# Token sums held behind each head's root, the last gate tile in the branches' banks, the small projection amid the first keys, and the decay's minimum in a row of its own

## The chip, the core and the metric

The kernel runs on one core of one Trainium2 chip. A core has a matrix engine (TensorE, "PE" in the profile, its weight loads "PEld"), VectorE (DVE), ScalarE (ACT), GpSimd (POOL) and SyncE (SP), each with an instruction stream of its own that runs in order, and 16 DMA engines. The metric is the device time of one execution in microseconds; less is better.

## The reference

One layer of a hybrid decoder: a norm, one wide projection, two token-mixing branches that are gated and merged, an output projection, and a gated FFN with a causal convolution. There are 1024 tokens of 1024 channels, and 16 meta tokens in front of them (1040 in all).

```python
proj = h @ w_in + b_in                 # queries, keys, values, gates, and the small columns g_lr, m_i, m_f
log_a = log_sigmoid(g_lr @ gla_w_gate + gla_b_gate) / 16
o_gla = gla_chunked(q, k, v, log_a)    # 4 heads: gated linear attention, chunks of 64 tokens
o_ml  = mlstm_chunked(mq, mk, mv, log_i, log_f)         # 4 heads: matrix memory
y = sigmoid(gate_a) * (o_gla @ w_branch_gla) + sigmoid(gate_b) * (o_ml @ w_branch_ml)
x1 = x + y @ w_out
out = rms_norm(x1 + (silu(conv(x1n @ w_up)[gate]) * conv(x1n @ w_up)[up]) @ w_down)
```

`log_sigmoid(z)` is worked out as min(z, 0) - ln(1 + exp(-|z|)). Each head's output goes through a norm of its own, which needs one number per token, (mean of squares + eps) to the power -1/2; that power is called the head's root here.

## The kernel before

Every float32 matrix product is made of three matmuls on split operands (high by high, low by high, high by low part). So a tile `wr_x` is a weight as it was loaded, `wH_x` its high part, which ACT writes, and `wL_x` the low part, which DVE writes (lines 109 and 110). `xH` and `xL` are the input, split the same way.

The kernel has stages. The heads stage runs to about 640 us: for head s = 0 to 7, `key_query_proj(s)` and `value_proj(s)` are the main stream of matmuls, and `main` lets the generators of the head before (`gla` for heads 0 to 3, `mlstm` for 4 to 7) and a closing generator `post` advance by 1.15 steps for each step of the main stream. `post` scales and turns a finished head's rows (`ot`, `of`), and stores them. Then come the gates (`piece`, tiles Vg, Xg, Yg, Zg and gu, to about 938 us), the two branches' products (`bg` and `bm`, to about 1126 us), the output projection, and the FFN. A tile scheduler sets each engine's order from the order of the code, from priorities (`hp`), and from `issue_after`, which holds an instruction in the schedule until a named one has been issued. Each engine then runs its list strictly in order, DMA issues included.

Around the change:

- A head's finish. DVE writes `rs{s}v` (line 91), POOL takes the root `rs{s}r` (line 93), and in heads 4 to 7 DVE multiplies the result by `rc` (line 937). On DVE the next in order behind that are the value tiles `v` (line 208), which read the matmuls of `value_proj` out of their PSUM banks.
- Token sums. `post` of heads 3 to 6 calls `token_sums`: eight POOL operations (lines 468 and 471) of 128x514 on tiles `xa` and `xb`, and eight DMA issues from POOL's queue (line 483) that store them for the FFN's stage. `half_load` and `half_sums` (lines 496 and 502) do the like for a piece of a weight. `xa` and `xb` take their buffers from a tag of two, which is also that of `KT`, the turned keys of the next head (lines 765 and 872).
- Decay. For heads 0 to 3 `decay` multiplies the small projection by the gate's weights into three PSUM tiles `pre` (128x346 or 348, from a tag of three buffers that the scores, the states and others share), ACT makes ln(1 + exp(-|z|)) in `la` in the steps Abs (line 620), Exp and Ln, DVE takes min(z, 0) - la from the PSUM tiles in three operations (line 624) and makes the running sum `bc` (line 627). From `bc` follow the factors `pk` of the scores `sc` of the first head, level by level.
- The small projection. `key_query_proj(0)` runs keys and queries of head 0 and keys of head 1 together, and then the small columns (`uk["lr"]`, weights `w_lr`) as 72 matmuls; `decay(0)` is called behind it.
- The last gate tile. `merge_gate_b(7)` (its matmuls are `pe`, its output `gb`) runs at the end of the gates stage, each third of it in a bank of its own (`pe7_0`, `pe7_342`, `pe7_684`), and ACT takes each third out with a copy (line 456). Then `load_o` loads the first branch's operand, of which ACT writes the high part `ogH` (line 1207, eight operations) and DVE the low part `ogL` (line 1208), and the branch's products start.

Of the kernel before, what the change touches and what calls it, by code (L numbers as in the profile page):

```python
# [17 lines left out]
P = 128  # L18
# [27 lines left out]
def hybrid_kernel(ctx, tc, x, meta, norm_mix, w_in, b_in, gla_w_gate, gla_b_gate, gla_norm,  # L46
# [38 lines left out]
    warm = const.tile([P, 1], F32, name="warm")  # L85
    nc.scalar.activation(warm, one1, AF.Exp)

    def rstd_of(ss, n, w, pool, name):

        v = pool.tile([P, w], F32, name=name + "v", tag="rv", bufs=4)  # L90
        nc.vector.tensor_scalar(v, ss, 1.0 / n, EPS, OP.mult, OP.add)
        r = pool.tile([P, w], F32, name=name + "r", tag="rr", bufs=4)
        nc.gpsimd.tensor_tensor(r, v, mhalf.to_broadcast([P, w]), OP.pow)
        return r


# [71 lines left out]
    def together(*gens):  # L168
        gens = list(gens)
        while gens:  # L170
            for g in list(gens):
                try:
                    next(g)
                except StopIteration:
                    gens.remove(g)
                    continue
                yield
# [232 lines left out]
    rsc = dram.tile([2, H, T], F32, name="rsc")  # L410

    heads = {}

    def key_proj(s):
        hh = heads.setdefault(s, {})
        kT = hh["k"] = hd.tile([P, T + 3], F32, name=f"kT{s}", tag="k", bufs=2)
        return proj_cm(uk[s], TH_ALL if s > 1 else SEG_ALL, 0, lambda p, t0, n: nc.scalar.activation(
            kT[:, t0:t0 + n], p, AF.Identity, bias=cc(C_GK + s)))

    def key_query_proj(s):  # L420
        h = s % 4
        hh = heads.setdefault(s, {})
        if s < 4:
            pk = key_proj(s) if s != 1 else iter(())
            qT = hh["q"] = hd.tile([P, T + 3], F32, name=f"qT{s}", tag="q", bufs=2)
            pq = proj_cm(uq[s], TH_POST if s else SEG_POST, T0, lambda p, t0, n: nc.scalar.activation(
                qT[:, t0:t0 + n], p, AF.Identity, bias=cc(C_GQ + h), scale=QS))
            if s == 0:
                yield from together(pk, pq, key_proj(1))
                yield from proj_cm(uk["lr"], TH_ALL, 0, lambda p, t0, n: nc.scalar.activation(  # L430
                    raw_s[0:96, t0:t0 + n], p[0:96, :], AF.Identity, bias=bsm[0:96]))
            else:
                yield from pk
                yield from pq
        else:
            kT = hd.tile([P, T + 3], F32, name=f"kT{s}", tag="k", bufs=2)
            qT = hd.tile([P, T + 3], F32, name=f"qT{s}", tag="q", bufs=2)
            hh["k"], hh["q"] = kT, qT
            for z, u, c in ((kT, uk[s], C_MK), (qT, uq[s], C_MQ)):
                nc.gpsimd.memset(z[:, 0:3], 0.0)  # L440
                yield from proj_cm(u, TH_ALL, 0, lambda p, t0, n, z=z, c=c: nc.scalar.activation(
                    z[:, 3 + t0:3 + t0 + n], p, AF.Identity, bias=cc(c + h)))
# [10 lines left out]
    def merge_gate_b(j, bank=None, st=None):  # L453
        if st is None:
            st = wp.tile([P, T], F32, name=f"gb{j}", tag="gst", bufs=1)
        yield from proj_cm(ugb[j], TH_POST, T0, lambda p, t0, n: nc.scalar.activation(
            st[:, t0:t0 + n], p, AF.Copy), bank)
        nc.scalar.dma_start(gsc["b"][j], st[:, :NP])
# [116 lines left out]
    def post(s, o, om, sc, ncols):  # L575

        h = s % 4
        g = "g" if s < 4 else "m"
        if 3 <= s < 7:
            stored = token_sums(s - 3)  # L580
        for c in range(NC):
            nc.scalar.activation(o(c), o(c), AF.Copy, scale=sc[:, c + 1:c + 2])
        nc.scalar.activation(om, om, AF.Copy, scale=sc[:2, 0:1])
        for _ in range(3 if s != 3 else 6):
            yield
        for j in range(2):
            of = hd.tile([P, T], F32, name=f"of{s}_{j}", tag="r", bufs=2)
            for gi in range(2):
                tp = ps.tile([P, 4, P], F32, name=f"ot{s}_{j}_{gi}", tag="s", bufs=3)
                for i in range(4):  # L590
                    nc.tensor.transpose(tp[:, i, :], o(4 * gi + i)[:, j * P:(j + 1) * P], ident)
                a, b = 2 + 512 * gi, 2 + 512 * (gi + 1)
                nc.scalar.activation(of[:, a:b], tp.rearrange("p n w -> p (n w)"), AF.Copy, scale=ncols[j])
                if gi == 0:
                    yield
                    if 3 <= s < 6:
                        if j == 0:
                            with tc.issue_after(stored.ins):
                                t = half_load(wp, "gst")
                        else:  # L600
                            half_sums(*t)
            tp = ps.tile([P, 4, P], F32, name=f"otm{s}_{j}", tag="s", bufs=3)
            nc.tensor.transpose(tp[:, 0, :2], om[:, j * P:(j + 1) * P], ident[:2, :2])
            nc.vector.tensor_scalar(of[:, 0:2], tp[:, 0, :2], ncols[j], None, OP.mult)
            nc.sync.dma_start(osc[g][2 * h + j], of[:, :NP])
            yield
# [5 lines left out]
    def decay(s):  # L612
        la = wtile(f"la{s}")
        pre = []
        for t0, n in TH_ALL:
            pt = ps.tile([P, 512], F32, name=f"pre{s}_{t0}", tag="s", bufs=3)
            nc.tensor.matmul(pt[:, :n], wg[:, P * s:P * (s + 1)], raw_s[0:NM + 1, t0:t0 + n], start=True, stop=True)
            pre.append((pt, la[:, t0:t0 + n], n))
        for pt, l, n in pre:
            nc.scalar.activation(l, pt[:, :n], AF.Abs)  # L620
        nc.scalar.activation(la, la, AF.Exp, scale=-1.0)
        nc.scalar.activation(la, la, AF.Ln, bias=one1)
        for pt, l, n in pre:
            nc.vector.scalar_tensor_tensor(l, pt[:, :n], 0.0, l, OP.min, OP.subtract)
        bc = wp.tile([P, T], F32, name=f"bc{s}", tag="gst", bufs=1) if s % 2 else \
            hd.tile([P, T], F32, name=f"bc{s}", tag="bc")
        nc.vector.tensor_tensor_scan(bc, rmask, la, 0.0, OP.mult, OP.add)
        heads.setdefault(s, {})["decay"] = la, bc

    def gla(s):  # L630
        h = s
        hh = heads[s]
        kT, qT, vt = hh["k"], hh["q"], hh["v"]
        kv, qv = kT[:, NM:T], qT[:, 2:NP]
        def lv(t, b):
            return t.rearrange("p (n h w) -> p n h w", h=2, w=b)
# [123 lines left out]
        for g in range(2):  # L760
# [3 lines left out]
                nc.tensor.transpose(tp[:, i, :], kh[:, NM + P * c:NM + P * (c + 1)], ident)  # L764
            nc.scalar.activation(KT[:, 512 * g:512 * g + 512], tp.rearrange("p a b -> p (a b)"), AF.Copy)
        yield

        def upd(c2):
            up = ps.tile([P, 2, DV], F32, name=f"up{s}_{c2}", tag="s", bufs=3)
# [168 lines left out]
        closing.append(post(s, o, om[:, :DV], sc, [cc(C_MN + 2 * h + j) for j in range(2)]))  # L938


    side, closing = [], []

    def step(gens):
        if gens:
            try:
# [15 lines left out]
    def main(gen, pace=PACE):  # L961
        for _ in gen:
            due[0] += pace
            while due[0] >= 1:
                due[0] -= 1
                advance()


    main(key_query_proj(0))
    decay(0)  # L970
    for s in range(8):
        side.append((gla if s < 4 else mlstm)(s))
        if s == 3:
            side.append(small_rows())
        main(value_proj(s))
        if s < 7:
            main(key_query_proj(s + 1))
# [141 lines left out]
    def row(name, tag, bufs=1):  # L1119
        return gs.tile([P, T], F32, name=name, tag=tag, bufs=bufs)  # L1120
# [18 lines left out]
    def gate_bank(name):  # L1139
        return lambda t0: psG.tile([P, 512], F32, name=f"{name}_{t0}", tag=f"{'XYZ'[t0 // 342]}1")  # L1140
# [42 lines left out]
    for j in END:  # L1183
        ugb[j] = u_cm(w_in, O_GB + P * j, f"gb{j}")
    gate_finish(NG - 1)
    for j in END:
        main(merge_gate_b(j, gate_bank(f"pe{j}"), row(f"gb{j}", "u0", 2)))
    gs_ctx.close()


# [22 lines left out]
    uo = [[[U.add(wsrc(w_o, 4 * g, 4, DV * n, DV), [P, 4, DV], f"wo{i}{n}{g}") for g in range(2)]  # L1213
           for n in range(4)] for i in range(2)]

    def prod3(u, X, kouter, name):
        wH, wL = U.get(u)
        pt = ps2.tile([P, 3, 512], F32, name=name, tag="big", bufs=2)
        XH, XL = X
        order = [(k, i) for k in range(NK) for i in range(3)] if kouter else [(k, i) for i in range(3) for k in range(NK)]  # L1220
        for k, i in order:
            t0, n = TH_POST[i]
            for a, b, j in ((wH, XH, 0), (wH, XL, 1), (wL, XH, 2)):
                nc.tensor.matmul(pt[:, i, :n], a[:, k, :], b[k][:, t0:t0 + n],  # L1224
                                 start=(k == 0 and j == 0), stop=(k == NK - 1 and j == 2))
        return pt[:, :, :342]

    def th(t):
        return t[:, :NP].rearrange("p (a b) -> p a b", a=3)

    r1_ctx.close()
    r1b_ctx = ctx.enter_context(ExitStack())
    r1b = r1b_ctx.enter_context(tc.tile_pool(name="r1b", bufs=1, reuse_waits="tile"))
    yg = []

    def merge_tile(j):
# [2 lines left out]

    merge_tile(0)  # L1240
    og, loaded, split = load_o("g", r2, "O", nc.gpsimd)
    hold(evicted["U"])
    U.get(ubg[0], 1)
    hold(split.ins)
# [622 lines left out]
```

## Time and profile before

| | |
|---|---|
| median of 3 runs | 1912.39 us (1908.16, 1912.39, 1912.55) |
| the profiled execution | 1907.36 us, of which the span is 1905.4 us |
| PE busy | 1863.9 us, 98% of the span |
| DVE, ACT, POOL busy | 1208.6, 853.3 and 418.0 us |

The span runs from the first to the last instruction that the profiler saw. Times are microseconds from its start. A row of waits gives how long an engine stood idle in total for a reason, how often, and the longest. A row of the timeline gives the start, the duration, the engine, the line, the operation, the tile written and those read, and in brackets how long the engine was idle before it and what released it.

### The profile page before, as it was taken

Reading aid. Unit: us, or ns where it says so; the run is one execution under the profiler, and the core shown is the slowest. Engines: PE = TensorE matmul, PEld = TensorE weight load, DVE = VectorE, ACT = ScalarE, POOL = GpSimd, SP = SyncE. Lnnn points to the kernel's source line nnn. Section 1 sums busy time; section 2 is a strip of 40 time slices with the busy share of each in tenths; the row PEclk is TensorE's granted clock in tenths of the full one; section 3 lists DMA queues with packets and bytes.
Section 4 is the critical chain, followed back from the end, with each engine's and each line's share of the span. In section 5 each row is a group of like instructions: output and inputs, shape, how many; then the busy total and the mean of one; then the engine's idle time right before and its main releaser. Section 6 shows DMA issues by size and latency. Waiting matters only on the chain. (4 is left out here: it accounts for less than half of the span.)

```text
span 1905.4 us, 32685 instructions
## 1 busy us (share of the span) xinstructions
PE 1863.9 (98%) x13377; PEld 1783.5 (94%) x13377; DVE 1208.6 (63%) x1777; ACT 853.3 (45%) x1371; POOL 418.0 (22%) x471
## 2 busy tenths in 40 slices
PE   8999999999999999999999999999999999999998
PEld 8889999999899999999899999999999999987876
DVE  6456456356653366565442555688878788796876
ACT  5345555545453443332331234544344343465664
POOL 3101111234431001125362610012232222200000
PEclk9999999999999999999999999999999999999999
DMA  5111021143333756665883653323433333288794
GB/s 168 34 37 59 12 70 43 30 145 97 93 91 89 181 119 167 167 160 174 276 275 124 202 194 125 122 79 111 128 117 106 106 111 118 93 301 326 284 370 166
DMA packets 221824, 270.02 MB, mean 142 GB/s; under 512 B 13742, under 2 KB 177088, under 8 KB 221675
## 3 DMA queue, kind: packets, MB, share of 16 engines
q1 hardware_dynamic: 200603, 199.93, 34.5%
q0 software_dynamic: 16928, 57.76, 9.2%
q10 hardware_dynamic: 4144, 10.26, 1.5%
q8 instruction: 105, 1.72, 0.4%
q14 instruction: 44, 0.36, 0.1%
HBM read 198.33 MB, written 69.57 MB: 141 GB/s over the span
## 5 line engine op out<-in xcount | busy, mean ns | idle before, releaser
L502 POOL TENSOR_TENSOR ts<-ts 128x256 f32<-128x256 f32 x88 | 82.4, 941 | 50.2 <-DMA ts<-in_ffn_w_down_dram 47.9
L1418 POOL TENSOR_TENSOR SB<-SA,rg 128x512 f32<-128x512 f32 x20 | 32.1, 1607 | 233.5 <-issue 114.1
L204 PE MATMUL pv<-wH_mv,xH 128*128 128x256 f32 x256 | 75.3, 294 | 1.5 <-DVE v L208 1.5
L204 PE MATMUL pv<-wH_gv,xH 128*128 128x256 f32 x256 | 75.2, 294 | 0.0
L1505 PE MATMUL po<-wH_wo,yH 128*128 128x256 f32 x256 | 72.7, 284 | 0.1
L204 PE MATMUL pv<-wH_gv,xL 128*128 128x256 f32 x256 | 72.5, 283 | 0.0
L204 PE MATMUL pv<-wL_gv,xH 128*128 128x256 f32 x256 | 72.1, 282 | 0.0
L204 PE MATMUL pv<-wL_mv,xH 128*128 128x256 f32 x256 | 72.0, 281 | 0.0
L1505 PE MATMUL po<-wL_wo,yH 128*128 128x256 f32 x256 | 71.7, 281 | 0.3 <-DVE wL_wo L110 0.3
L1505 PE MATMUL po<-wH_wo,yL 128*128 128x256 f32 x256 | 71.9, 282 | 0.0
L204 PE MATMUL pv<-wH_mv,xL 128*128 128x256 f32 x256 | 71.9, 281 | 0.0
L710 POOL TENSOR_TENSOR pk<-pk,kT 128x256 f32<-128x256 f32 (+1 forms) x24 | 30.6, 1278 | 175.0 <-ACT pk L708 159.9
L1453 DVE SCALAR_TENSOR_TENSOR cv<-u,fc,cv 128x1024 f32<-128x1024 f32 x44 | 65.3, 1484 | 0.4
L1224 PE MATMUL bg<-ogH,wH_bg 128*128 128x342 f32 x192 | 61.9, 324 | 3.0 <-ACT ogH L1207 3.0
L1400 POOL TENSOR_TENSOR A<-u2raw,A 128x512 fp32r<-128x512 f32 x20 | 43.9, 2194 | 92.7 <-ACT A L1399 92.7
L1224 PE MATMUL bg<-ogL,wH_bg 128*128 128x342 f32 x192 | 61.9, 324 | 0.7 <-DVE ogL L1208 0.7
L1224 PE MATMUL bg<-ogH,wL_bg 128*128 128x342 f32 x192 | 61.9, 323 | 0.0
L1224 PE MATMUL bm<-omH,wH_bm 128*128 128x342 f32 x192 | 61.4, 320 | 0.0
L1224 PE MATMUL bm<-omH,wL_bm 128*128 128x342 f32 x192 | 61.3, 319 | 0.0
L1224 PE MATMUL bm<-omL,wH_bm 128*128 128x342 f32 x192 | 61.2, 319 | 0.0
L208 DVE TENSOR_TENSOR v<-pv,bB 128x256 f32<-128x256 f32 x64 | 26.6, 419 | 51.5 <-PE pv L204 51.5
L1743 POOL TENSOR_TENSOR fr<-fv,mhalf 128x1 f32<-128x1 f32 x8 | 4.7, 595 | 227.3 <-DVE fv L1741 227.3
(753 smaller groups left out, 7510.4 us busy)
## 6 DMA issues: line engine op xcount, KB each, us to landing
gw<-in_w_in_dram SPq DMA_DIRECT2D x26, 512.0 KB
ts<-in_ffn_w_down_dram POOLq DMA_DIRECT2D x44, 256.0 KB, 4.3
tdn<-ts POOLq DMA_DIRECT2D x44, 256.0 KB, 3.2
rg<-in_ffn_w_up_dram SPq DMA_DIRECT2D x22, 512.0 KB
ru<-in_ffn_w_up_dram SPq DMA_DIRECT2D x22, 512.0 KB
adr<-s SPq DMA_DIRECT2D x40, 256.0 KB
rd<-in_ffn_w_down_dram SPq DMA_DIRECT2D x20, 512.0 KB
do<-tdn SPq DMA_DIRECT2D x18, 512.0 KB
```

The source lines that it names most:

```text
L204: nc.tensor.matmul(pt[:, :DV], a[:, k, t0:t0 + P], b[:, k % 4, :], start=(i == 0), stop=(i == 3 * NK - 1))
L208: nc.vector.tensor_tensor(vt[:n, c, :DV], pt[:n, :DV], bB[:n, :], OP.add)
L502: nc.gpsimd.tensor_tensor(t[:, o], t[:, a], t[:, b], OP.subtract)
L710: eng.tensor_tensor(e, e, k, OP.mult)
L1224: nc.tensor.matmul(pt[:, i, :n], a[:, k, :], b[k][:, t0:t0 + n], start=(k == 0 and j == 0), stop=(k == NK - 1 and j == 2))
L1400: eng.tensor_tensor(l, src, h.bitcast(F32), OP.subtract)
L1418: late.tensor_tensor(sb[:, 0:4], sa[:, 0:4], rg[:, 0:4], OP.subtract)
L1453: nc.vector.scalar_tensor_tensor(y, u[:, j:SEQ + j], fc[:, j, jj:jj + 1], y, OP.mult, OP.add)
L1505: nc.tensor.matmul(pt[:, :DV], a, b[:, k % 4, :], start=(k == 0 and i == 0), stop=(k == NK - 1 and i == len(terms) - 1))
L1743: nc.gpsimd.tensor_tensor(rs, v, mhalf, OP.pow)
```

## The change

Four edits.

1. `rstd_of` keeps its last root in `rooted`, and `token_sums` is called under `issue_after` of that root. On POOL's list the sums and their stores stood ahead of the root of the head that was finishing; now they stand behind it. The loads of `half_load`, which wait in the schedule for the sums' last store, move with them.
2. The last gate tile is made with `prod3`, in one tile of three banks in the pool of the branches' products, behind the gates stage, and `load_o` is called ahead of it. ACT takes it out with one copy of 128x1026, held behind the last `ogH`, and not with three of 128x342.
3. In the first head the small projection is run after six of the first segments of keys and queries, and `decay(0)` after one more; `gla(0)` joins the side stream ahead of the last segments of head 1's keys. `gla` takes its value tiles later, where it needs them.
4. In `decay` DVE writes min(z, 0) from each PSUM tile straight to `bc` as soon as the matmul is done, and later subtracts `la` with one operation of 128x1040 from SBUF to SBUF.

```diff
+    rooted = []
...
-        nc.gpsimd.tensor_tensor(r, v, mhalf.to_broadcast([P, w]), OP.pow)
+        rooted[:] = [nc.gpsimd.tensor_tensor(r, v, mhalf.to_broadcast([P, w]), OP.pow)]
         return r
...
-                yield from together(pk, pq, key_proj(1))
+                k1 = key_proj(1)
+                yield from islice(together(pk, pq, k1), 6)
                 yield from proj_cm(uk["lr"], TH_ALL, 0, lambda p, t0, n: nc.scalar.activation(
                     raw_s[0:96, t0:t0 + n], p[0:96, :], AF.Identity, bias=bsm[0:96]))
+                pkq = together(pk, pq)
+                yield from islice(pkq, 1)
+                decay(0)
+                yield from pkq
+                side.append(gla(0))
+                yield from k1
...
         if 3 <= s < 7:
-            stored = token_sums(s - 3)
+            with tc.issue_after(rooted[0].ins):
+                stored = token_sums(s - 3)
...
-            pre.append((pt, la[:, t0:t0 + n], n))
-        for pt, l, n in pre:
-            nc.scalar.activation(l, pt[:, :n], AF.Abs)
+            pre.append((pt, t0, n))
+        bc = wp.tile([P, T], F32, name=f"bc{s}", tag="gst", bufs=1) if s % 2 else \
+            hd.tile([P, T], F32, name=f"bc{s}", tag="bc")
+        for pt, t0, n in pre:
+            nc.scalar.activation(la[:, t0:t0 + n], pt[:, :n], AF.Abs)
+            nc.vector.tensor_scalar(bc[:, t0:t0 + n], pt[:, :n], 0.0, None, OP.min)
         nc.scalar.activation(la, la, AF.Exp, scale=-1.0)
         nc.scalar.activation(la, la, AF.Ln, bias=one1)
-        for pt, l, n in pre:
-            nc.vector.scalar_tensor_tensor(l, pt[:, :n], 0.0, l, OP.min, OP.subtract)
-        bc = wp.tile([P, T], F32, name=f"bc{s}", tag="gst", bufs=1) if s % 2 else \
-            hd.tile([P, T], F32, name=f"bc{s}", tag="bc")
+        nc.vector.tensor_tensor(la, bc, la, OP.subtract)
         nc.vector.tensor_tensor_scan(bc, rmask, la, 0.0, OP.mult, OP.add)
...
     gate_finish(NG - 1)
-    for j in END:
-        main(merge_gate_b(j, gate_bank(f"pe{j}"), row(f"gb{j}", "u0", 2)))
     gs_ctx.close()
...
+    merge_tile(0)
+    og, loaded, split = load_o("g", r2, "O", nc.gpsimd)
+    for j in END:
+        pt = prod3(ugb[j], [[t[:, k] for k in range(NK)] for t in (xH, xL)], False, f"pe{j}", 0, T0)
+        gb = r2.tile([P, T], F32, name=f"gb{j}", tag="hn", bufs=1)[:, :NP]
+        with tc.issue_after(split.ins):
+            nc.scalar.activation(th(gb), pt, AF.Copy)
+        nc.scalar.dma_start(gsc["b"][j], gb)
     r1_ctx.close()
...
-    merge_tile(0)
-    og, loaded, split = load_o("g", r2, "O", nc.gpsimd)
```

The changed kernel's line numbers are 2 to 15 higher at the places shown below. POOL's list at the end of head 5, before (`rs5r` is the root, `xa2` and `xb2` the third set of token sums, `tsc` where they are stored, `ts10` a piece of a weight that `half_load` fetches):

```order
L471 TENSOR_TENSOR xa2_5108<-xa2_5108,xb2_5109 128x514
L483 DMA tsc258_426<-xb2_5109 128x258
L483 DMA tsc256_427<-xb2_5109 128x256
L483 DMA tsc258_426<-xa2_5108 128x258
L483 DMA tsc256_427<-xa2_5108 128x256
L483 DMA tsc258_426<-xa2_5108 128x258
L483 DMA tsc256_427<-xa2_5108 128x256
L496 DMA ts10_5248<-in_ffn_w_down_dram 128x2x256 x2
L93 TENSOR_TENSOR rs5r_5070<-rs5v_5068,mhalf_81 128x9
L449 MEMSET v7_5417 128x9
```

and after:

```order
L514 DMA tdn1_429<-ts01_4658 256x1x256
L459 MEMSET v7_5488 128x9
L95 TENSOR_TENSOR rs5r_4996<-rs5v_4994,mhalf_81 128x9
L478 TENSOR_TENSOR xa2_5034<-xH_87,xL_88 128x514 x2
L478 TENSOR_TENSOR xb2_5035<-xH_87,xL_88 128x514
L481 TENSOR_TENSOR xb2_5035<-xa2_5034 128x514
L481 TENSOR_TENSOR xa2_5034<-xb2_5035,xa2_5034 128x514
L478 TENSOR_TENSOR xa2_5034<-xH_87,xL_88 128x514
```

The root has passed the whole set of sums, their eight stores and the two loads of `ts10`. ACT's list from the last gate products to the first branch products, before (`wH_bg1` is a branch weight, `yg0` the first gate of the merge):

```order
L109 ACTIVATE wH_bg1_9597<-wr_bg1_9595 128x1024
L1131 DMA gscb_424<-gu012_9236 128x1026
L1131 DMA gscb_424<-gu112_9237 128x1026
L456 ACTIVATE gb7_9461<-pe7_0_9468 128x342
L456 ACTIVATE gb7_9461<-pe7_342_9494 128x342
L456 ACTIVATE gb7_9461<-pe7_684_9520 128x342
L458 DMA gscb_424<-gb7_9461 128x1026
L1251 ACTIVATE yg0_9559<-yg0_9559,col_104 128x1026
L1207 ACTIVATE ogH0_9561<-ogL0_9563 128x1026 x4
L1207 ACTIVATE ogH1_9562<-ogL1_9564 128x1026 x4
L109 ACTIVATE wH_bg2_9603<-wr_bg2_9601 128x1024
```

and after:

```order
L1142 DMA gscb_424<-gu112_9241 128x1026
L1266 ACTIVATE yg0_9473<-yg0_9473,col_104 128x1026
L1216 ACTIVATE ogH0_9475<-ogL0_9477 128x1026 x4
L1216 ACTIVATE ogH1_9476<-ogL1_9478 128x1026 x4
L111 ACTIVATE wH_bg2_9603<-wr_bg2_9601 128x1024
L1252 ACTIVATE gb7_9582<-pe7_9509 128x1026
L1266 ACTIVATE yg1_9607<-yg1_9607,col_104 128x1026
```

The copies of the last gate tile stood ahead of `ogH`; the one copy now stands behind all eight and behind `wH_bg2`. DVE's list at the first head's decay, before (`pv4` are value products, `gv0` and `gq1` weights of values and queries):

```order
L110 TENSOR_TENSOR wL_gv0_0_760<-wr_gv0_0_757,wH_gv0_0_759 128x1024
L110 TENSOR_TENSOR wL_gv0_1_766<-wr_gv0_1_763,wH_gv0_1_765 128x1024
L110 TENSOR_TENSOR wL_gq1_870<-wr_gq1_867,wH_gq1_869 128x1024
L624 SCALAR_TENSOR_TENSOR la0_847<-pre0_0_848,la0_847 128x348
L197 TENSOR_TENSOR vlo4_896<-pv4_0_879,vlo4_896 16x256
L624 SCALAR_TENSOR_TENSOR la0_847<-pre0_348_850,la0_847 128x346
L198 TENSOR_TENSOR v0_866<-vlo4_896,bB0_864 16x256
L624 SCALAR_TENSOR_TENSOR la0_847<-pre0_694_852,la0_847 128x346
L208 TENSOR_TENSOR v0_866<-pv4_1_906,bB0_864 128x256
L627 SCALAR_TENSOR_TENSOR bc0_862<-rmask_92,la0_847 128x1040
```

and after:

```order
L634 TENSOR_SCALAR bc0_724<-pre0_0_718 128x348
L634 TENSOR_SCALAR bc0_724<-pre0_348_720 128x346
L634 TENSOR_SCALAR bc0_724<-pre0_694_722 128x346
L637 TENSOR_TENSOR la0_717<-bc0_724,la0_717 128x1040
L638 SCALAR_TENSOR_TENSOR bc0_724<-rmask_92,la0_717 128x1040
L717 TENSOR_TENSOR pk0_2_845<-bc0_724 128x128x2
L717 TENSOR_TENSOR pk0_2_845<-bc0_724 128x4x32x2
L718 TENSOR_TENSOR pk0_2_845<-bc0_724 128x512
L717 TENSOR_TENSOR pk0_4_879<-bc0_724 128x64x4
L112 TENSOR_TENSOR wL_gv0_0_604<-wr_gv0_0_601,wH_gv0_0_603 128x1024
```

The decay now stands ahead of the three weights' low parts and of the first value tiles; those low parts fall between the levels' factors `pk`.

More of the change, by code (lines that the diff above doesn't have):

```diff
@@ L412, in hybrid_kernel @@
     heads = {}
+    side, closing = [], []
     def key_proj(s):
@@ L632, in gla @@
         hh = heads[s]
-        kT, qT, vt = hh["k"], hh["q"], hh["v"]
+        kT, qT = hh["k"], hh["q"]
         kv, qv = kT[:, NM:T], qT[:, 2:NP]
@@ L766, in gla @@
         yield
+        vt = hh["v"]
         def upd(c2):
@@ L938, in mlstm @@
         closing.append(post(s, o, om[:, :DV], sc, [cc(C_MN + 2 * h + j) for j in range(2)]))
-    side, closing = [], []
     def step(gens):
@@ L969, in hybrid_kernel @@
     main(key_query_proj(0))
-    decay(0)
     for s in range(8):
-        side.append((gla if s < 4 else mlstm)(s))
+        if s:
+            side.append((gla if s < 4 else mlstm)(s))
         if s == 3:
@@ L1214, in hybrid_kernel, with prod3 @@
            for n in range(4)] for i in range(2)]
-    def prod3(u, X, kouter, name):
-        wH, wL = U.get(u)
+    def prod3(u, X, kouter, name, ahead=2, base=0):
+        wH, wL = U.get(u, ahead)
         pt = ps2.tile([P, 3, 512], F32, name=name, tag="big", bufs=2)
@@ L1223, in prod3 @@
             for a, b, j in ((wH, XH, 0), (wH, XL, 1), (wL, XH, 2)):
-                nc.tensor.matmul(pt[:, i, :n], a[:, k, :], b[k][:, t0:t0 + n],
+                nc.tensor.matmul(pt[:, i, :n], a[:, k, :], b[k][:, base + t0:base + t0 + n],
                                  start=(k == 0 and j == 0), stop=(k == NK - 1 and j == 2))
@@ L1229, in th @@
         return t[:, :NP].rearrange("p (a b) -> p a b", a=3)
-    r1_ctx.close()
-    r1b_ctx = ctx.enter_context(ExitStack())
-    r1b = r1b_ctx.enter_context(tc.tile_pool(name="r1b", bufs=1, reuse_waits="tile"))
     yg = []
@@ L1241, in hybrid_kernel @@
     og, loaded, split = load_o("g", r2, "O", nc.gpsimd)
+    for j in END:
[4 more added lines that the diff above has]
+        nc.scalar.dma_start(gsc["b"][j], gb)
+    r1_ctx.close()
+    r1b_ctx = ctx.enter_context(ExitStack())
+    r1b = r1b_ctx.enter_context(tc.tile_pool(name="r1b", bufs=1, reuse_waits="tile"))
     hold(evicted["U"])
```

## The prediction

> **What bounds the kernel now.** I read the page first:
>
> ```profile
> span 1905.4 us, 32685 instructions
> PE 1863.9 (98%) x13377; PEld 1783.5 (94%) x13377; DVE 1208.6 (63%) x1777; ACT 853.3 (45%) x1371; POOL 418.0 (22%) x471
> ```
>
> PE is the bound, and the change removes no matmul from it. What can be won is PE's idle time, 41.5 us in all, and the time that it ran at a lower clock. So the second view was PE's waits (the total, how often, the longest):
>
> ```profile
> PE pj L161 <- DVE v L208: 4.8, 2, 2.4
> PE bg L1224 <- ACT ogH L1207: 3.0, 1, 3.0
> PE u L780 <- DVE la L624: 2.8, 3, 1.1
> PE sc L661 <- DVE pk L711: 2.7, 2, 1.7
> PE pv L204 <- DVE v L208: 1.5, 1, 1.5
> PE bg L1224 <- DVE ogL L1208: 0.7, 1, 0.7
> PE sc L661 <- POOL pk L710: 0.5, 1, 0.5
> ```
>
> These seven rows, 16.0 us, are the waits that the four edits can touch. The third view was the timeline around each.
>
> **Edit 1, the roots.** POOL's and DVE's rows at the end of head 5:
>
> ```profile
> 521.46 1.84 POOL L93 TENSOR_TENSOR rs5r<-rs5v,mhalf 128x9 f32<-128x9 f32 x1
> ...
> 518.57 0.17 DVE L91 TENSOR_SCALAR rs5v<-ss 128x9 f32<-128x9 f32 x1
> 523.33 0.17 DVE L937 TENSOR_TENSOR rs5r<-rs5r,rc 128x9 f32<-128x9 f32 x1 [4.45 <-POOL rs5r L93]
> 523.41 0.75 DVE L208 TENSOR_TENSOR v<-pv,bB 128x256 f32<-128x256 f32 x2
> ```
>
> The root's input is there at 518.74, but POOL still has the sums' stores and two loads ahead of it in its list, and starts the root 2.7 us later. DVE stands at line 937, and behind it in order stand the value tiles whose banks PE needs: one of the two `pj` waits of 2.4. With the root ahead of the sums, line 937 can run at 518.74 + 1.84 = 520.6 and the first value tile is out at 521.1; now it is out at 523.8. That is 2.7 earlier against a stall of 2.4: the stall goes, -2.4. At the end of head 6:
>
> ```profile
> 570.52 4.92 DVE L851 SCALAR_TENSOR_TENSOR wt<-MB,tcol,big 128x128 f32<-128x128 f32 x4
> 575.43 0.60 DVE L851 SCALAR_TENSOR_TENSOR wt<-MB,tcol,big 128x128 f32<-128x128 f32 x2
> 577.03 0.17 DVE L91 TENSOR_SCALAR rs6v<-ss 128x9 f32<-128x9 f32 x1
> 580.08 0.17 DVE L937 TENSOR_TENSOR rs6r<-rs6r,rc 128x9 f32<-128x9 f32 x1 [2.88 <-POOL rs6r L93]
> ```
>
> The same gives line 937 at 579.0, 1.1 earlier. But the four `wt` of 1.23 each ran beside the sums; the next ones after them on DVE take 0.3 (0.60 for two), so without sums there `rs6v` comes some 3 us earlier too. The 1.5 wait of `pv` goes: -1.5.
>
> The other `pj` wait of 2.4 ends at head 3's finish, and DVE was not idle there:
>
> ```profile
> 376.21 3.31 DVE L526 TENSOR_TENSOR_SCAN sr<-sr,raw_s 4x1040 f32<-4x1040 f32 x1
> 380.68 2.32 DVE L529 TENSOR_TENSOR_SCAN sr<-rmask,sr 4x1040 f32<-4x1040 f32 x1
> 383.03 2.13 DVE L838 SCALAR_TENSOR_TENSOR kc<-kT,col,kc 128x1040 f32<-128x1040 f32 x1
> 385.08 0.41 DVE L208 TENSOR_TENSOR v<-pv,bB 128x256 f32<-128x256 f32 x1
> 386.25 1.30 DVE L838 SCALAR_TENSOR_TENSOR kc<-kT,col,kc 128x1040 f32<-128x1040 f32 x1
> 387.59 1.23 DVE L533 TENSOR_TENSOR sr<-raw_s,sr 4x1040 f32<-4x1040 f32 x1
> ```
>
> Scans and `kc` stretch from 2.32 to 3.31 and from 1.30 to 2.13 beside the sums. The value tile stands behind them. After the change the sums start only after this root, so the first scan is 1.0 shorter, but the second and `kc` may still be stretched. Bounds: -2.4 (nothing stretched) and 0. I take the middle, -1.2.
>
> A shortened idle also bears on the clock:
>
> ```profile
> 380.00:392.00 12.00, 9.58 (x56) 9.34 (x56) 11.24 (x11) 6.96 (x13) 10.79 (x14) 0.86 0.32 106
> 515.00:530.00 15.00, 12.57 (x85) 12.29 (x84) 7.59 (x19) 9.02 (x16) 13.62 (x17) 1.00 0.57 172
> 943.00:947.00 4.00, 4.00 (x17) 4.00 (x18) 4.00 (x4) 4.00 (x5) 0.74 (x2) 0.57 1.03 323
> 947.00:970.00 23.00, 23.00 (x148) 23.00 (x148) 13.56 (x12) 11.06 (x12) 7.29 (x11) 1.00 1.05 380
> ```
>
> The last numbers of a row are the granted clock, the DMA share and the traffic. Behind the wait at 383 the clock fell to 0.86 over 12 us, that is 12 x 0.14 = 1.7 us of work; behind the equal wait at 521 it did not fall; at 943 to 947 it fell to 0.57, 1.7 us again. So a wait of 2.4 costs 1.7 more in one case of two here. Halving the one at 383 probably saves that: bounds -1.7 and 0, and -1.2 taken. By the Trainium skill ("TensorE: Matmul & The Clock Gate", section "What's actually happening") the clock is halved only after a whole idle window of about 3.4 us, on a free-running grid. By that rule none of these waits would lose clock and the sum would be 2.9 smaller; the rows above disagree (2.4 sufficed once), so the sum keeps the two terms, and the rule's free-running grid agrees with one equal wait being punished and the other not.
>
> The edit adds a wait. `xa` and `xb` share buffers with `KT` of the next head, which must wait until the sums' stores have landed:
>
> ```profile
> L483 POOL DMA_DIRECT2D tsc<-xa x16: 539/542/592, 386.9 to 577.6; - x16
> L471 POOL TENSOR_TENSOR xa<-xa,xb x4: 1308/1314/2916, 381.1 to 573.7; 128x514 f32<-128x514 f32 x4
> DMA to landing us min/median/max: 2.1/2.6/5.2
> ...
> 538.13 1.45 DVE L872 TENSOR_TENSOR KT<-kt,tcol 128x512 f32<-128x512 f32 x2
> 592.90 1.44 DVE L872 TENSOR_TENSOR KT<-kt,tcol 128x512 f32<-128x512 f32 x2
> ```
>
> A set of sums takes 8 x 1.31 + 8 x 0.54 = 14.8. Behind the root (0.2 + 1.84) and with a landing of 2.6 the buffers are free 19.5 after `rs{s}v` starts. `KT` of head 7 starts 592.90 - 577.03 = 15.9 behind `rs6v` now, less the 1.5 of stall that goes, plus the 3 by which `rs6v` comes earlier: 17.4, so it is 2.1 late. For head 6 it is 538.13 - 518.57 = 19.6, less 2.4, plus perhaps 3: 20.2, just in time. Behind `KT` on DVE stand the masked scores and the value tiles, so PE feels it if it has nothing in hand. I take half of 2.1 and round up, +1.2; bounds 0, and with every sum stretched to 2.92 as above, 8 x 1.6 = 12.9 more per head: for two heads 12.2 + 15.0 = 27.
>
> Edit 1: -2.4 - 1.5 - 1.2 - 1.2 + 1.2 = -5.1.
>
> **Edit 2, the last gate tile.**
>
> ```profile
> 927.88 0.42 DVE L1027 TENSOR_TENSOR gu<-Zg,gu 128x256 f32<-128x256 f32 x1 [0.18 <-PE Zg L990]
> ...
> 938.55 0.46 ACT L456 ACTIVATE gb<-pe 128x342 f32<-128x342 f32 x1 [3.33 <-PE pe L161]
> 939.41 1.15 ACT L1251 ACTIVATE yg<-yg,col 128x1026 f32<-128x1026 f32 x1 [0.40 <-ACT gb L456]
> 940.47 7.69 ACT L1207 ACTIVATE ogH<-ogL 128x1026 fp32r<-128x1026 f32 x8
> 950.41 1.06 ACT L109 ACTIVATE wH_bg<-wr_bg 128x1024 fp32r<-128x1024 f32 x1 [2.25 <-DMA wr_bg<-in_w_branch_gla_dram]
> ```
>
> Now `ogH` begins behind the gate's copies, and the branch's first matmuls wait 3.0 + 0.7 for it and lose 1.7 of clock behind that. With those copies out of the way `ogH` runs under the gate tile's own 72 matmuls, about 11 us, as its inputs land: -5.4. Against that, the first four matmuls of `pe`, which now fill a wait for `gu` (4 x 0.16 = 0.6), can no longer do so (0.16 is 23.00 / 148 of the last windows row), and all of `pe` waits for the whole three-bank tile. The last `gu` frees it: it starts at 927.88, right after PE's last `Zg`, and ends at 928.30, so PE stands about 0.6 there. With 0.3 for the hand-over that is +1.5 (bounds +0.7 and +2.5). The copy of the gate tile then stands behind eight `ogH` and `wH_bg2`; the second branch product `bg1` takes the tile's buffer and would start about 951 (its 72 matmuls at 0.16 behind those of `pe` and `bg0`, from 928.4). `wH_bg2` is done at 951.47 by the row above, and the copy takes about 1.15 (the `yg` row, the same shape): up to 1.3 late if the landing stays where it is. The transfers in this stretch have a DMA share of 1.05, so it may come no earlier. I take +0.3, since the loads' issues move ahead with `load_o`. Edit 2: -5.4 + 1.5 + 0.3 = -3.6.
>
> **Edits 3 and 4, the small projection and the decay.**
>
> ```profile
> 75.42 0.52 DVE L624 SCALAR_TENSOR_TENSOR la<-pre,la 128x348 f32<-128x348 f32 x1 [14.60 <-ACT la L622]
> 53.21 1.23 DVE L110 TENSOR_TENSOR wL_gv<-wr_gv,wH_gv 128x1024 fp32r<-128x1024 f32 x1 [13.97 <-ACT wH_gv L109]
> L161 PE MATMUL pj<-xH,w_lr x48: 314/322/327, 57.7 to 69.0; 128*128 128x346 f32 x32, 128*128 128x348 f32 x16
> ```
>
> The 72 matmuls of the small projection (48 of these and 24 on `xL`, 57.6 to 69.1) move ahead of segments of keys and queries, so the decay's chain starts some 14 us sooner, and the first scores are due sooner too, by about 64 matmuls of value work that now follow them. What DVE must do ahead of the scores grows: three `wL` of 1.23, which ran in its idle time (14 us before the first), fall between the levels, 3.7; against that no value tiles (0.4 each) stand in the chain. The 3.2 of `sc` waits may go, or become 3.2 + 3.7 - 0.4 x 4 = 5.3: bounds -3.2 and +2.1. Taken: 0.
>
> In each of four decays DVE does three minimum operations (like the 0.50 of line 624) and one subtraction of 128x1040 (the SBUF row of that length above, 1.23), where it did three of 0.50: +1.23, beside PE's work, since the scan's start moves by 1.23 - 1.5. What goes is that the PSUM tiles `pre` were held until ACT's Ln was done (DVE idle 14.6 ahead of its first read above): `u`'s tile waited for them three times, 2.8. With the minimum right behind the matmul, -2.5 (bounds -2.8 and 0, if DVE's list reaches the minimum late).
>
> [...]
>
> **The sum.** -5.1 - 3.6 + 0 - 2.5 = -11.2. The side stream of all heads moves some 50 matmuls forward, and new short waits of the size of the smallest above (0.5 to 0.7) come in perhaps three places: +2. Total -9.2. Against the profiled execution: 1907.36 - 9.2 = 1898.2. The median of the runs is 5.0 above that execution, so the median becomes about 1903. A difference under 0.3%, 5.7 us, cannot be told from none here; the bounds are 1906.7 and 1918.1.
>
> **Rivals.**
> - *The forecast*: waits go as priced, 1898 to 1906.6. Chance 0.54.
> - *Slower: `KT` waits for the late sums.* Place: the start of heads 6 and 7. Price 0 to 27; without my 1.2 the time is 1902, so it is slower from 16 us on, that is with sums at about 2.2 us each; with all at 2.92, 1929. For it: `wt` and `kc` stretch beside sums; against it: 1.31 is the median. Chance 0.12 (0.08 slower, 0.04 same).
> - *The first head's chain.* All of 3.7 + 1.23 falls on the path: 1903 + 4.9 = 1908. For it: DVE works without a break in that chain. Chance 0.13 (0.08 same).
> - *POOL and DVE lock out each other at the new places.* Each of four subtractions waits for a POOL operation (1.31), and the stall at 383 stays with its clock: 1903 + 5.2 + 2.4 = 1910.6. The stretched rows speak for it; against it, POOL is busy 22% only. Chance 0.12 (0.08 same). [...]
> - *Edit 1 does not do it*: value tiles late for another reason. Without its -5.1 the time is 1908. DVE's idle 4.45 right at the root speaks against it. Chance 0.05 (0.03 same).
> - Something unlisted, slower: 0.04.
>
> Faster 0.54 + 0.05 + 0.04 + 0.02 = 0.65, same 0.23, slower 0.12. The range is 1897 (the good bounds of edits 1, 2 and 4 and half of edit 3's: -8.0 - 4.7 - 2.8 - 1.6 + 2 = -15.1) to 1912, which leaves out the `KT` rival's upper half and what is unlisted.
>
> **What would show it.** Right: no `pj` wait for `v` at 521 and no `pv` wait; roots within 0.5 of `rs{s}v`; no `bg` wait for `ogH` and no fall of the clock at 943; no `u` wait for `la`. Wrong: `KT` or DVE behind it waiting on `tsc` stores; `sc` waits above 5; `bg` waiting for `gb`'s copy by more than 1.3; `pe` waiting over 2.

## The result, and the profile after

The changed kernel takes 1899.23 us (median of 6 runs, 1897.74 to 1904.83) against 1910.69 us for the kernel before (6 runs, 1908.16 to 1912.55): a ratio of 0.9946, 95% interval 0.9931 to 0.9961. In a later comparison, beside other kernels, it was 0.9957 (0.9945 to 0.9969). So it is faster by about half a per cent, 8 to 11 us; the forecast was 9.2 us, a median of 1903 and a range of 1897 to 1912.

The profiled executions differ by 9.6 us of span. The page of the kernel after:

```profile
span 1895.8 us, 32688 instructions
PE 1859.8 (98%) x13377; PEld 1779.6 (94%) x13377; DVE 1214.4 (64%) x1781; ACT 854.0 (45%) x1369; POOL 424.5 (22%) x471
```

PE's idle time fell from 41.5 to 36.0 us, 5.5, and its busy time by 4.1 with the same number of matmuls; most of that is clock, since two falls of 1.7 us are gone (below). PE's waits after, those that answer to the ones shown of before (total, times, longest):

```profile
PE pj L163 <- DVE v L210: 2.6, 2, 1.5
PE po L1520 <- DVE yM L1301: 2.4, 1, 2.4
PE ot L602 <- ACT of L604: 1.9, 2, 1.6
PE pv L206 <- DVE v L210: 1.8, 2, 1.0
PE rtp L578 <- ACT of L604: 1.7, 1, 1.7
PE sc L672 <- DVE pk L722: 1.6, 1, 1.6
PE Yg L1001 <- DVE gu L1031: 1.0, 1, 1.0
PE pe L1233 <- DVE gu L1038: 0.6, 1, 0.6
```

The reader should see three things. The rows `bg` for `ogH` and `ogL` and `u` for `la` are gone, 6.5 us in all. The rows `pj` and `pv` for a value tile are still there, 4.4 in place of 6.3, but their place is another one. And there is a row that nobody asked for: the first output product `po`, 2.4 us.

The ends of the heads, VectorE's and GpSimd's rows at the end of head 5:

```profile
509.28 0.17 DVE L93 TENSOR_SCALAR rs5v<-ss 128x9 f32<-128x9 f32 x1
511.41 1.25 DVE L950 TENSOR_TENSOR rs5r<-rs5r,rc 128x9 f32<-128x9 f32 x1 [1.82 <-POOL rs5r L95]
...
509.54 1.83 POOL L95 TENSOR_TENSOR rs5r<-rs5v,mhalf 128x9 f32<-128x9 f32 x1 [2.89 <-DVE rs5v L93]
511.35 2.54 POOL L478 TENSOR_TENSOR xa<-xH,xL 128x514 f32<-128x514 f32 x2
```

The root starts 0.1 behind its input and the sums stand behind it, as was meant. (The product `rs5r` on VectorE now meets the first sum and takes 1.25 where it took 0.17; PE does not feel it.) PE has no wait at all from 500 to 620 us. At the end of head 3 it is otherwise:

```profile
374.11 1.34 DVE L200 TENSOR_TENSOR v<-vlo,bB 16x256 f32<-16x256 f32 x1
375.38 0.41 DVE L210 TENSOR_TENSOR v<-pv,bB 128x256 f32<-128x256 f32 x1
375.81 1.34 DVE L541 COPY sr<-sr 4x1040 f32<-4x1040 f32 x1
377.19 2.23 DVE L851 SCALAR_TENSOR_TENSOR kc<-kT,col,kc 128x1040 f32<-128x1040 f32 x1
381.58 2.33 DVE L547 TENSOR_TENSOR sr<-sr,sr 4x1040 f32<-4x1040 f32 x1
385.63 2.22 DVE L552 TENSOR_TENSOR sr<-sr,sr 4x1024 f32<-4x1024 f32 x1
390.85 1.30 DVE L851 SCALAR_TENSOR_TENSOR kc<-kT,col,kc 128x1040 f32<-128x1040 f32 x1
...
369.08 3.79 POOL L95 TENSOR_TENSOR rs3r<-rs3v,mhalf 128x9 f32<-128x9 f32 x1 [8.58 <-DVE rs3v L93]
382.77 2.28 POOL L478 TENSOR_TENSOR xa<-xH,xL 128x514 f32<-128x514 f32 x1
```

All four `pj` and `pv` waits, the `rtp` wait and 0.2 of `ot` lie here, between 374 and 404: 6.3 us where one wait of 2.4 was before. VectorE works without a break until 396, and most of its operations between SBUF tiles take nearly twice their time while the sums run. The clock, in rows of windows (the third number from the end):

```profile
0.00:20.00 20.00, 13.84 (x65) 12.35 (x66) 15.41 (x39) 11.79 (x22) 3.89 (x12) 0.74 0.90 289
370.00:420.00 50.00, 43.60 (x309) 41.81 (x308) 34.41 (x44) 22.78 (x33) 28.98 (x26) 1.00 0.56 141
900.00:960.00 60.00, 58.36 (x409) 57.99 (x408) 27.74 (x31) 25.03 (x28) 22.06 (x34) 1.00 0.92 305
```

Both falls of before, behind 383 and at 943, are gone; the six shorter waits of head 3 did not halve it. In the first 20 us, where PE waits for its input anyway, this execution ran at 0.74.

### The profile page after: what moved, and what is told of

Read it like the earlier page. It is cut to its first block, busy times and chain, and to the rows that moved or that the text cites. A ratio compares the mean times of both kernels' runs of the same rounds, so it can differ in the third digit from the quotient of the medians.

```text
span 1895.8 us, 32688 instructions
## 1 busy us (share of the span) xinstructions
PE 1859.8 (98%) x13377; PEld 1779.6 (94%) x13377; DVE 1214.4 (64%) x1781; ACT 854.0 (45%) x1369; POOL 424.5 (22%) x471
```

## The experiments

Each kernel was run beside the kernel before on the same chip. Ratios are to that kernel; the changed kernel stands at 0.9946 and 0.9957 on this scale, and an interval is about 0.0015 to either side. A single edit is worth 0.001 to 0.003, so the time alone seldom decides, and PE's waits do.

**The edits undone one at a time**

First edit 1, the roots:

```diff
-            with tc.issue_after(rooted[0].ins):
-                stored = token_sums(s - 3)
+            stored = token_sums(s - 3)
```

> The changed kernel with edit 1 undone: the token sums stand ahead of the roots again. My theory: the waits for value tiles at the ends of heads 5 and 6 (2.4 and 1.5 us) come back, nothing else of weight moves, so it is slower than the changed kernel by about 4 us (1903). Rival: edit 1 also made the cluster of six waits at the end of head 3 (6.3 us in the changed kernel, one of 2.4 before), because the sums now run beside the small rows' work on VectorE; then undoing it gives 3.9 back and takes 3.9, and the time is that of the changed kernel within 2 us, with a cluster at head 3 of about 2.4.

1900.89 us, 0.9963 (0.9948 to 0.9978). PE's waits at the ends of heads 5 and 6:

```profile
PE pv L206 <- DVE v L210: 3.0, 1, 3.0
PE pv L206 <- DVE rc L945: 2.2, 1, 2.2
```

5.2 us came back there, and the clock fell behind the second of them (the last section has the row); the cluster at head 3 went from 6.3 to 0.6. The rival holds, with other sizes: the edit took 5.2 of waits in one place and cost 5.7 in another. The gates' first product starts at 658.7 us with and 658.8 without it. So in these two executions, with the other three edits in place, edit 1 as a whole was worth nothing up to the end of the heads, and head 3's 2.4 of before would have been 0.6 without it. (Of the 2.8 by which this execution's span is longer, 1.8 came later, from the clock behind the `po` wait; the last section has that row too.) The time is 0.0006 to 0.0017 above the changed kernel, 1 to 3 us, which the intervals do not separate from none.

Edit 2, the last gate tile put back at the end of the gates (its matmuls in `gate_bank`, `load_o` behind them):

```diff
     gate_finish(NG - 1)
+    for j in END:
+        main(merge_gate_b(j, gate_bank(f"pe{j}"), row(f"gb{j}", "u0", 2)))
     gs_ctx.close()
...
     merge_tile(0)
     og, loaded, split = load_o("g", r2, "O", nc.gpsimd)
-    for j in END:
-        pt = prod3(ugb[j], ...)
```

> The changed kernel with edit 2 undone: the last gate tile again in banks of its own at the gates' end. My theory: the waits for ogH and ogL (3.0 + 0.7) and the slow clock behind them (1.7) come back, against 1.1 less waiting ahead of pe, so plus 4.3; and the new wait of 2.4 at the first output product goes, since the number of tiles that take turns in the two three-bank buffers is even again and the last branch tile is in the other banks: net plus 1.9 (1901). Rival: the wait at the output product has another cause (a late yM); then it stays, and the kernel is slower by 4.3 (1903.5).

1902.13 us, 0.9964 (0.9950 to 0.9978). The waits:

```profile
PE bg L1235 <- ACT ogH L1218: 3.0, 1, 3.0
PE bg L1235 <- DVE ogL L1219: 0.7, 1, 0.7
PE pe L163 <- ACT gu L1030: 0.5, 1, 0.5
```

The clock over 900 to 960 is 0.97 again, and there is no `po` wait for `yM`. That is the first theory: the new `po` wait belongs to edit 2. The time is 0.0007 to 0.0018 above the changed kernel, 1.3 to 3.4 us, where 1.9 was expected.

Edit 3, the small projection behind all keys and queries again, with `decay(0)` and `gla(0)` where they were:

```diff
-                k1 = key_proj(1)
-                yield from islice(together(pk, pq, k1), 6)
+                yield from together(pk, pq, key_proj(1))
...
-                decay(0)
...
+    decay(0)
     for s in range(8):
```

> The changed kernel with edit 3 undone: the small projection behind all first keys and queries. My theory: sc waits of 1.65 become about 3.2, and the wait of ot for of in the first head (1.65, new in the changed kernel) goes: within 1 us of the changed kernel (1899). Rival: the earlier side stream is what keeps the ends of the heads free (ot 0.9, pc 0.3) and what brought small rows' work on top of head 3's end; then the cluster at head 3 gets smaller by 2 to 4 us and waits of about 1.2 come back at the heads' end: 1896 to 1898.

1902.06 us, 0.9971 (0.9961 to 0.9981). `sc` waits 2.9 us (2.4 for VectorE and 0.5 for GpSimd) where the changed kernel waits 1.6; `ot` waits 0.9 at the heads' end, in place of 1.6 in the first head; `Yg` waits 2.2 and not 1.0. At head 3 the cluster is 3.8 us, and the clock fell behind it (0.97 over 370 to 420). So neither theory holds as it was put: the cluster is smaller by 2.5 without edit 3, as the rival said, but what came back elsewhere and the clock cost more.

Edit 4, the minimum behind ACT's logarithm again:

```diff
-            nc.vector.tensor_scalar(bc[:, t0:t0 + n], pt[:, :n], 0.0, None, OP.min)
...
-        nc.vector.tensor_tensor(la, bc, la, OP.subtract)
+        for pt, l, n in pre:
+            nc.vector.scalar_tensor_tensor(l, pt[:, :n], 0.0, l, OP.min, OP.subtract)
```

> The changed kernel with edit 4 undone: the minimum again in the operation behind ACT's logarithm, from PSUM. My theory: three waits of u for a bank (0.8, 1.0, 1.1) and one of op (0.3) come back: slower by 2.8 to 3.1 (1902). Rival: the subtraction from two SBUF tiles costs VectorE and GpSimd what the waits cost; then it is within 1 us of the changed kernel.

1900.35 us, 0.9959 (0.9944 to 0.9974). By the time it cannot be told from the changed kernel; by the profile the three waits of `u` came back:

```profile
PE u L793 <- DVE la L635: 2.2, 3, 0.8
```

The subtraction takes 1.24 us in all four decays of the changed kernel, which is what it takes alone, so the rival (a price paid to GpSimd) did not happen.

**The cluster at head 3**

Head 3's sums alone put back ahead of the root:

```diff
-            with tc.issue_after(rooted[0].ins):
+            with tc.issue_after(rooted[0].ins) if s > 3 else nullcontext():
                 stored = token_sums(s - 3)
```

> The changed kernel with the sums of head 3 alone back in their old place, ahead of its root; heads 4 to 6 as changed. Theory (from the kernel without edit 1, where the waits at the end of head 3 were 0.6 in all and not 6.3): the cluster at head 3 goes and the waits at the ends of heads 5 and 6 stay away, so 5 to 6 us faster than the changed kernel. Rival: the cluster moves to a later head, since POOL's work is only shifted; then within 2 us of it.

1892.71 us, 0.9923 (0.9908 to 0.9937): 0.0023 to 0.0034, or 4.4 to 6.5 us, under the changed kernel. The waits at head 3 are 0.6, and those of heads 5 and 6 stay away. The first theory holds. It does not say why the sums hurt there; the next kernel does. It holds head 3's sums behind the small rows with a real dependence:

```diff
-        nc.vector.tensor_tensor(d[:, :NM - 1], a[:, :NM - 1], M[...].to_broadcast([4, NM - 1]), OP.subtract)
+        rows_done[:] = [nc.vector.tensor_tensor(d[:, :NM - 1], a[:, :NM - 1], M[...].to_broadcast([4, NM - 1]), OP.subtract), d]
...
+        if s == 3:
+            with tc.issue_after(rooted[0].ins), tc.issue_after(rows_done[0].ins):
+                scr = hd.tile([P, 1], F32, name="scr")
+                gate = nc.gpsimd.tensor_tensor(scr[96:100], rows_done[1][:, 0:1], rows_done[1][:, 1:2], OP.add)
+            with tc.issue_after(gate.ins):
+                stored = token_sums(0)
```

> The changed kernel with the sums of head 3 held, by a small GpSimd operation that reads the small rows' last result, until VectorE has done the small rows. If the cluster at head 3 comes from sums and small rows slowing each other, each side runs at its own pace: VectorE's rows there go back to 2.3 (scan), 1.3 (kc), 1.2 (subtractions), the cluster falls from 6.3 to under 2, and it is 4 us or more faster than the changed kernel. Rival: VectorE simply has too much work ahead of the value tiles there, whatever POOL does; then the cluster stays above 4.

1892.70 us, 0.9917 (0.9902 to 0.9932). VectorE's rows of the same operations, and GpSimd's:

```profile
374.15 0.41 DVE L200 TENSOR_TENSOR v<-vlo,bB 16x256 f32<-16x256 f32 x1
374.93 0.69 DVE L543 COPY sr<-sr 4x1040 f32<-4x1040 f32 x1
375.66 1.30 DVE L859 SCALAR_TENSOR_TENSOR kc<-kT,col,kc 128x1040 f32<-128x1040 f32 x1
378.49 1.22 DVE L549 TENSOR_TENSOR sr<-sr,sr 4x1040 f32<-4x1040 f32 x1
380.79 1.22 DVE L554 TENSOR_TENSOR sr<-sr,sr 4x1024 f32<-4x1024 f32 x1
...
384.15 1.24 POOL L602 TENSOR_TENSOR scr<-sr 4x1 f32<-4x1 f32 x1 [11.23 <-DVE sr L566]
385.47 4.60 POOL L478 TENSOR_TENSOR xa<-xH,xL 128x514 f32<-128x514 f32 x2
```

The same instructions in the same order on VectorE, without sums beside them, take 0.41, 1.30, 1.22 and 1.22 (those with two SBUF inputs) where they took 1.34, 2.23, 2.33 and 2.22: about 1.0 less each, a little under the 1.3 that one of GpSimd's sums takes. The value tile that reads PSUM and one SBUF tile stayed at 0.41 in both. The cluster falls to 0.4. This shows the cause: the sums and the small rows block each other, and the value tiles stand behind the small rows. Once the rows are done, the sums stretch the next VectorE work instead, but no value tile that PE needs soon stands behind that. By the Trainium skill ("SBUF — State Buffer", section "Who interferes with whom") VectorE and GpSimd exclude each other from a shared pair of ports for a whole operation where VectorE reads two SBUF inputs and GpSimd reads SBUF too; the four pairs of durations agree. These are not the only case: the copy, which has one SBUF input, went from 1.34 to 0.69 as well, and in the profile of before `rs3v`, also with one, took 0.75 beside a sum where `rs5v` took 0.17.

**The wait at the first output product**

```diff
     psF = ctx.enter_context(tc.tile_pool(name="psF", bufs=1, space=PSUM, reuse_waits="tile"))
+    for tag in ("V1", "Y1", "Z1"):
+        nc.vector.memset(psF.tile([P, 512], F32, name=f"first{tag}", tag=tag)[:, :1], 0.0)
```

> The changed kernel with the first three output products placed in the banks of the last branch tile but one (three tiny writes claim the other banks first). If the new wait of 2.4 at the first output product comes from the banks, it goes, and the kernel is 2.4 faster (and spared a fall of the clock where that wait caused one). Rival: yM, ACT or the weights are late there; then a wait of about 2 stays.

1897.25 us, 0.9945 (0.9929 to 0.9962): 0 to 2.3 us under the changed kernel, so the time does not decide. The matmul in question and VectorE's last read of the last branch tile, in the changed kernel and then here:

```profile
1115.81 0.51 DVE L1297 TENSOR_TENSOR sb<-bm,sb 128x342 f32<-128x342 f32 x1
1116.46 0.36 PE L1520 MATMUL po<-wH_wo,yH 128*128 128x256 f32 x1 [2.39 <-DVE yM L1301]
```

```profile
1115.10 0.32 PE L1233 MATMUL bm<-omH,wL_bm 128*128 128x342 f32 x1
1115.26 0.28 PE L1522 MATMUL po<-wH_wo,yH 128*128 128x256 f32 x1
...
1117.15 0.51 DVE L1297 TENSOR_TENSOR sb<-bm,sb 128x342 f32<-128x342 f32 x1
1117.58 0.15 DVE L1301 TENSOR_TENSOR yM<-sb,yM 128x2 fp32r<-128x2 f32 x1
```

The wait is gone. The two three-bank buffers take turns; with the gate tile in that pool there are 17 tiles and not 16, so the last branch tile sits in banks 0 to 2 and not 3 to 5, and the first output products had been given banks 0 to 2. `yM` was only the last thing that VectorE did before; the release was the banks: with other banks the product starts 2.3 us ahead of `yM`. Of the 2.4, 1.1 was lost to a wait of `Xg` in the gates, ahead of the mended place, that this profile has and the changed kernel's has not. The kernel with the sums doubled (below) has the same wait without the mended banks, and the kernels with both repairs lack it; what brings it stays open.

**How much room `KT` has**

In the changed kernel VectorE waits for the sums' stores once, at head 7:

```profile
581.16 1.29 DVE L885 TENSOR_TENSOR KT<-kt,tcol 128x512 f32<-128x512 f32 x2 [1.39 <-DMA tsc<-xb]
```

To find how far this is from PE's path, the sums of heads 5 and 6 were done twice (the second time with the same values):

```diff
+        for _ in range(2 if k > 1 else 1):
             whole(a[1], k, second)
...
```

> The changed kernel with the eight token-sum operations of heads 5 and 6 done twice (the same values), 10.5 us more on POOL behind each of those roots. It measures the slack of KT, the rival by which I had the change slower. KT of head 6 would come about 10 us later, of head 7 about 12 (VectorE already waits 1.4 for it). If PE has 3 us in hand there, it waits some 7 at head 6 and 8 at head 7, 15 in all; if the rival was wrong in kind (KT is not on PE's path), PE waits under 3 in all.

1921.85 us in a single run. PE's waits there:

```profile
PE otm L615 <- DVE KT L886: 13.0, 2, 7.7
PE msc L893 <- DVE KT L886: 0.7, 2, 0.3
```

The two `otm` waits are 5.4 and 7.7 us. Of 10.5 us more of sums (8 x 1.31) PE felt 5.7 at head 6 and 8.0 at head 7, `msc` counted in, so by this estimate it has 4.8 and 2.5 in hand there. With these 13.7 us of waits the clock was 0.93 over 500 to 640, 9.8 us of work; together they make nearly all of the 24.1 by which the span is longer. So the rival is real in kind: `KT` is on PE's path as soon as the sums are 2.5 to 5 us later than now.

**Both repairs together**

The changed kernel again, in the same rounds as the next two:

> The changed kernel again, on the chip and in the rounds of the next two, as their yardstick: 0.9946 of the kernel before, as in the first comparison, with a cluster of six waits (6.3 us) at the end of head 3 and a wait of 2.4 at the first output product.

1900.10 us, 0.9957 (0.9945 to 0.9969). Then head 3's sums behind the small rows, and the banks:

> The changed kernel with head 3's sums behind the small rows and with the output products' banks put right. If the two costs are independent, they add up: 6 and 1.3 to 2.4 us under the changed kernel, 7 to 8 together (about 0.9905 of the kernel before). Rival: work that comes earlier meets the next stage's loads (as a wait of 1.1 did in the gates where the banks alone were mended) and half of it is lost: 4 us, 0.9925.

1889.43 us, 0.9906 (0.9891 to 0.9921), 10.7 under the changed kernel in the same rounds. What is left of the rows shown above:

```profile
PE ot L610 <- ACT of L612: 1.7, 1, 1.7
PE sc L680 <- DVE pk L730: 1.7, 1, 1.7
PE Yg L1009 <- DVE gu L1039: 1.0, 1, 1.0
PE pe L1241 <- DVE gu L1046: 0.6, 1, 0.6
```

The two costs add up: 5.9 (6.3 less 0.4) and 2.4 of waits make 8.3, and the `Xg` wait is not there. The 2.4 us beyond that lie within the intervals. And the third, with head 3's sums ahead of the root, and the banks:

> The same with head 3's sums in their old place, ahead of the root, and not behind the small rows. The waits of the two placings differed by 0.5 us, so the same time within 1 us is expected; if the sums ahead of the root cost more once the rest is tight, it is 2 us slower than the other.

1890.43 us, 0.9906 (0.9893 to 0.9920): the same time. Both are faster than both kernels, by about 0.9% and 0.5%.

## Why the prediction was right, and where it was not

The direction, the time and the range held; that the sum came so close is luck. The sum promised 5.1 us too much for the wait at head 3 and 1.7 for edit 2, and about 6 us made up for that: gains that were forecast smaller or not at all, a loss (`KT`) that did not come, and 2 us kept for new waits. By its terms:

- *Roots at heads 5 and 6, -2.4 and -1.5:* shown. The waits are gone, and undoing the edit brought back 5.2.
- *The wait at 383, -1.2:* wrong in sign. It became 6.3 where it was 2.4, plus 3.9. The step that failed was the choice of the middle between "nothing stretched" and "no gain": the bounds stopped at 0. I had the stretched rows on the page (2.32 to 3.31, 1.30 to 2.13) and counted on a first scan that would be shorter, but did not follow on where the sums would lie. Ahead of the root, part of them ran before the small rows; behind it, all eight fell on the small rows, with a value tile behind each second or third operation of VectorE. With edit 3 undone the waits there were 3.8 and not 6.3. The runs show -1.8 if head 3's sums are left where they were.
- *The clock there, -1.2:* measured -1.7; the wait of 2.4 had become several shorter ones.
- *`KT`, +1.2:* PE lost nothing; VectorE waited 1.4 (2.1 was worked out), and PE had room.
- *Edit 2, -3.6:* the waits 3.7 and the clock 1.7 went, 1.1 came back ahead of `pe` (1.6 where 0.5 was), and `bg1` did not wait: -4.3. Not seen at all: the turn of the buffers, plus 2.4 at the first output product, which leaves -1.9. The prediction spoke of which tile would take the gate tile's buffer next, but not of the last one.
- *Edit 3, 0:* `sc` waits fell by 1.6 against bounds of -3.2 and +2.1; `ot` moved from the heads' end (0.9) to the first head (1.6). The run without the edit was 0.0014 to 0.0025 above the changed kernel, some 3 to 5 us. A wait of `Yg` of 1.7 in the gates, which I had taken as untouched, is gone after the change; 1.2 of it came back in that run.
- *Edit 4, -2.5:* 2.8 in the profile, 2.2 when undone.
- *New short waits, +2:* there are such (`rtp`, `sct`, `ot`); all but 0.4 of `sct` is counted above.

Of the rivals, mutual blocking of VectorE and GpSimd came true at head 3 and not at the subtractions, where GpSimd was idle. I gave it 0.12, and it cost 3.9 where I had allowed 2.4 at that place. The stretched rows had been in view; the place where VectorE's work between SBUF tiles and GpSimd's sums would meet was the thing to look up in the two orders.

## What to carry to other kernels

When an edit moves a block of work behind a wait that it used to delay, look at what the other engine does in the new place, operation by operation: the end of one head here had 20 us of VectorE work in it and the others had not, and an exception for that one head was worth more than the rule. A tile added to a pool whose buffers take turns shifts every later tile by one, and the price shows where the pool ends. Read an order "held behind" as a place in a list: only a dependence holds work back on the chip.

## What the runs showed of the hardware

The same wait of PE halves the clock in one execution and not in the next. The wait of 2.4 us ahead of the first output product stands in eight profiles, at the same place of the program. The changed kernel and then the one without edit 1, over the 30 us around it:

```profile
1110.00:1140.00 30.00, 27.61 (x224) 27.16 (x223) 10.97 (x21) 8.77 (x23) 0.00 (x0) 1.00 0.31 106
```

```profile
1110.00:1140.00 30.00, 27.61 (x210) 27.15 (x209) 10.55 (x20) 8.27 (x21) 0.00 (x0) 0.94 0.31 107
```

PE is busy for 27.61 us in both, and gets through 14 matmuls fewer in the second: 30 x 0.06 = 1.8 us. The clock fell in four of the eight (without edits 1, 3 and 4, and with the sums doubled) and not in the other four. By the Trainium skill ("TensorE: Matmul & The Clock Gate", section "What's actually happening") it takes a whole idle window of about 3.4 us on a free-running grid; the runs disagree with the length, since 2.4 us sufficed, and are in keeping with the grid. The length of the wait did not decide within one execution either. In the kernel without edit 1 the clock stayed full behind the wait of 3.0 at 511 and fell behind the one of 2.2 at 564:

```profile
505.00:530.00 25.00, 22.03 (x160) 21.13 (x159) 9.58 (x26) 12.10 (x21) 13.83 (x17) 1.00 0.51 158
560.00:570.00 10.00, 7.79 (x53) 7.62 (x52) 7.58 (x21) 3.09 (x7) 8.19 (x10) 0.83 0.30 105
```

So a wait of 2.4 us was worth about 3.3 on the mean of the eight (an estimate: 2.4 and half of 1.8), and shorter ones were spared the difference: six waits of 0.2 to 1.7 us within 30 us at head 3 left the clock at 1.00.

VectorE operations on four partitions hold GpSimd back too: the root `rs3r`, 128x9, took 3.79 us beside the small rows' scans, and `rs5r` 1.83 where VectorE was idle.
